# Register loops of eight heads for the load and relay programs of an attention-times-values kernel

## The chip, the cores and the metric

The kernel runs on one core of one Trainium2 chip. The metric is the device time of one execution in microseconds. Each time quoted is the median of several executions; all were in the undisturbed state (none over 1.5% above the fastest of its kernel) unless said otherwise. In the views of the profile PE is TensorE, DVE VectorE, ACT ScalarE, POOL GpSimd and SP SyncE; L129 is line 129 of the kernel. A load *lands* when its semaphore has counted all of it, and a buffer's *release* is the end of the transposes that read it.

## The reference

```python
def setup_inputs():
    batch, n_heads, seq, head_dim = 8, 12, 1024, 64
    return {
        "attn_weights": np.random.randn(batch, n_heads, seq, seq).astype(np.float32),
        "v": np.random.randn(batch, n_heads, seq, head_dim).astype(np.float32),
    }

def reference(attn_weights, v):
    return np.einsum('bhqs,bhsd->bhqd', attn_weights, v).astype(np.float32)
```

There are 96 products of a 1024 x 1024 matrix of weights with a 1024 x 64 matrix v. The weights alone are 402.65 MB, and each is used once per column of v.

## The kernel before

A *unit* is half the rows of four heads, so the 96 heads make 48 units, and *four* units are eight heads. GpSimd loads a unit's weights as one transfer of 8.39 MB, cast to bf16 on the way, into one of two buffers `abf`. TensorE transposes the unit in sixteen groups, VectorE and ScalarE copy the transposes to `at`, TensorE multiplies them by v, transposes the product back, and the copies of it go to `osb`, from where they are stored. A load for unit n + 2 may be issued when unit n has been transposed. TensorE, VectorE and ScalarE already run register loops; GpSimd and SyncE are written out. The parts that the change touches:

```python
def load_attn(n):                       # on GpSimd
    pieces = [(0, G)] if n < HALVED else [(0, GH), (GH, GH)]
    for g0, gn in pieces:
        pool.dma_start(
            out=abf[n % 2][:, ds(g0, gn)].rearrange("p g s -> p (g s)"),
            in_=attn_q[n // 2][:, ds((n % 2 * G + g0) * S, gn * S)],
        ).then_inc(s_abf[n % 2] if g0 == 0 else s_second[n], 16)
...                                     # cut: load_v, store
load_attn(0)
load_attn(1)
...                                     # cut: constants
for n in range(NU - 2):                 # NU = 48; written out
    q, i = n // 2, n % 2
    if i == 0 and q % 2 == 1 and q + 1 < NV:
        for s in s_sp:
            pool.wait_ge(s, 2 * q + 2)
        load_v((q + 1) // 2)
    pool.wait_ge(s_t[True], (n + 1) * PER_DVE)    # unit n is transposed
    load_attn(n + 2)
    if i == 0 and q % 2 == 0 and 0 < q <= HELD_FROM:
        store_2(q - 2)
```

SyncE waits for each load and passes its landing on to TensorE, which asks for it in the middle of the unit (`s_half`):

```python
for n in range(-2, NU - 2):             # written out
    if n + 2 < HALVED:
        nc.sync.wait_ge(s_abf[n % 2], 16 * ((n + 2) // 2 + 1))
    else:
        nc.sync.wait_ge(s_second[n + 2], 16)
    nc.sync.sem_inc(s_half)
    ...                                 # cut: the same for v (s_vr) and for stores (s_free)
```

Of the kernel before, what the change touches and what calls it, by code (L numbers as in the profile page):

```python
# [10 lines left out]
def kernel(  # L11
# [18 lines left out]
    nc = tc.nc  # L30
# [4 lines left out]
    B, H, Q, S = attn_weights.shape  # L35
# [5 lines left out]
    G = Q // VP // 2  # L41
# [5 lines left out]
    NV = NH // VH  # L47
    NU = 2 * NV


    HELD_FROM = NV - 8
    BY_SYNC = NV - 4

    RING = 5
    NO = 2 * RING

    HALVED = NU - 2

    def slot(q):
        return q % NO  # L60

    attn_q = attn_weights.rearrange("b (hq four) (p r) s -> (b hq) (four p) (r s)", four=VH, p=VP)
    out_q = out.rearrange("b (hq four) (p r) d -> (b hq) (four p) (r d)", four=VH, p=VP)
    out_2 = out.rearrange("b h q d -> (b h) q d").rearrange(
        "(hq two four) (p r) d -> hq (four p) two (r d)", two=2, four=VH, p=VP
    )
    v_2 = v.rearrange("b h q d -> (b h) q d").rearrange(
        "(hq two four) (p r) d -> hq (four p) two (r d)", two=2, four=VH, p=VP
    )

    def on_dve(g):
        return g % 8 in (0, 2, 4, 5, 7)
# [5 lines left out]
    PER_DVE = sum(on_dve(g) for g in range(G))  # L78
    PER_ACT = G - PER_DVE

    with tc.tile_critical(no_gpsimd_drain=True):  # L81
        sem = tc.alloc_semaphore
# [3 lines left out]
        abf = [sb(f"abf{i}", [P, G, S], bf16) for i in range(2)]  # L86
        at = sb("at", [P, G, KW, P, 2], bf16)
        vr = sb("vr", [P, 2, VB, SB * D], bf16)
        vbf = sb("vbf", [P, SB, VH, D], bf16)
        ot = sb("ot", [P, GH, P], fp32)  # L90
        osb = sb("osb", [P, NO, 2 * G, D], fp32)
# [8 lines left out]
        s_abf = [sem(f"s_abf{i}") for i in range(2)]  # L100
        s_second = {n: sem(f"s_second{n}") for n in range(HALVED, NU)}
        s_v0, s_v = sem("s_v0"), sem("s_v")
        s_osb = [sem(f"s_osb{i}") for i in range(2)]
        s_held, s_end = sem("s_held"), sem("s_end")

        s_t = {True: sem("s_t_dve"), False: sem("s_t_act")}
        s_sp = [sem("s_sp_dve"), sem("s_sp_act")]
# [8 lines left out]
        s_out, s_fin = sem("s_out"), [sem("s_fin0"), sem("s_fin1")]  # L116
        s_memset, s_const, s_vr = sem("s_memset"), sem("s_const"), sem("s_vr")

        s_half, s_free = sem("s_half"), sem("s_free")
# [192 lines left out]

        pool = nc.gpsimd

        def load_attn(n):
            pieces = [(0, G)] if n < HALVED else [(0, GH), (GH, GH)]
            for g0, gn in pieces:
# [4 lines that stand above are left out]

        def load_v(iv):
            pool.dma_start(  # L324
                out=vr.rearrange("p two b x -> p two (b x)"), in_=v_2[iv]
            ).then_inc(s_v, 16)

        def store(q, fours, eng, done):
            eng.wait_ge(s_out, 2 * (q + fours) + 1)
            at_slot = osb[:, ds(slot(q), fours)].rearrange("p n r d -> p n (r d)")  # L330
            eng.dma_start(  # L331
                out=out_2[q // 2] if fours == 2 else out_q[q],
                in_=at_slot if fours == 2 else at_slot[:, 0],
                **({"single_packet": True} if eng is pool else {}),
            ).then_inc(done, 16)

        def store_2(q):
            store(q, 2, pool, s_osb[q // 2 % 2] if q < HELD_FROM else s_held)

        load_attn(0)  # L340
        load_attn(1)
        pool.wait_ge(s_memset, 2)
        pool.affine_select(
            out=ident,
            in_=ident,
# [7 lines left out]
        for h in range(VH):  # L353
            pool.wait_ge(s_const, h + 1)
            pool.affine_select(  # L355
                out=spread[ds(h * VP, VP)],
                in_=spread[ds(h * VP, VP)],
# [3 lines left out]
                pattern=[[1, VB], [-1, P]],  # L361
                channel_multiplier=VB,
            ).then_inc(s_const)
        for n in range(NU - 2):
            q, i = n // 2, n % 2
            if i == 0 and q % 2 == 1 and q + 1 < NV:
                for s in s_sp:
                    pool.wait_ge(s, 2 * q + 2)
                load_v((q + 1) // 2)
            pool.wait_ge(s_t[True], (n + 1) * PER_DVE)  # L370
            load_attn(n + 2)
            if i == 0 and q % 2 == 0 and 0 < q <= HELD_FROM:
                store_2(q - 2)
        for q in range(HELD_FROM, BY_SYNC, 2):
            store_2(q)
        pool.drain()


# [4 lines left out]
        for two, p0, pn in ((0, 0, P), (1, 0, 96), (1, 96, 22), (1, 118, 10)):  # L383
            nc.sync.dma_start(  # L384
                out=v32_2[ds(p0, pn), two], in_=v_2[0][ds(p0, pn), two]
            ).then_inc(s_v0, 16)
        nc.sync.sem_inc(s_free, RING)
        for n in range(-2, NU - 2):

            if n + 2 < HALVED:  # L390
                nc.sync.wait_ge(s_abf[n % 2], 16 * ((n + 2) // 2 + 1))
            else:
                nc.sync.wait_ge(s_second[n + 2], 16)
            nc.sync.sem_inc(s_half)
            if n >= 0 and n % 2 == 0:
                q = n // 2
                if q % 2 == 1 and q + 1 < NV:
                    nc.sync.wait_ge(s_v, 16 * ((q + 1) // 2))
                    nc.sync.sem_inc(s_vr, 2)
                if q % 2 == 1 and 1 < q <= HELD_FROM:  # L400
                    nc.sync.wait_ge(s_osb[(q - 3) // 2 % 2], 16 * ((q - 3) // 4 + 1))
                    nc.sync.sem_inc(s_free)
        store(NV - 4, 2, nc.sync, s_end)
        store(NV - 2, 1, nc.sync, s_end)
        rows = osb[:, slot(NV - 1)].rearrange("p (u half j) d -> p u half j d", u=2, half=2)
# [3 lines left out]
        for k in range(2):  # L409
            nc.sync.wait_ge(s_fin[k], 1)  # L410
            js = ds(4 * k, 4)
            nc.sync.dma_start(out=outs[:, 1, :, js], in_=rows[:, 1, :, js]).then_inc(s_end, 16)
        for k in range(2):
            nc.sync.wait_ge(s_osb[k], 16 * (HELD_FROM // 4))
        nc.sync.wait_ge(s_held, 16 * (BY_SYNC - HELD_FROM) // 2)
        nc.sync.wait_ge(s_end, 16 * 5)

# [29 lines left out]
```

## Time and profile before

| | before |
|---|---|
| time, median of 6 | 1055.07 us (1054.65 to 1055.70) |
| profile's span | 1053.1 us |
| busy share: TensorE, VectorE, ScalarE, GpSimd | 70%, 37%, 39%, 4% |
| bytes over the span | 452.99 MB, 430 GB/s |
| weight load, from issue to landing | 33.3 us |

Second, the row of instruction fetches among the DMA queues, which is to be compared after:

```profile
q14 instruction: 3, 0.02, 0.0%
```

### The profile page before, as it was taken

Reading aid. Unit: us, or ns where it says so; the run is one execution under the profiler, and the core shown is the slowest. Engines: PE = TensorE matmul, PEld = TensorE weight load, DVE = VectorE, ACT = ScalarE, POOL = GpSimd, SP = SyncE. Lnnn points to the kernel's source line nnn. Section 1 sums busy time; section 2 is a strip of 40 time slices with the busy share of each in tenths; the row PEclk is TensorE's granted clock in tenths of the full one; section 3 lists DMA queues with packets and bytes.
Section 4 is the critical chain, followed back from the end, with each engine's and each line's share of the span. In section 5 each row is a group of like instructions: output and inputs, shape, how many; then the busy total and the mean of one; then the engine's idle time right before and its main releaser. Section 6 shows DMA issues by size and latency. Waiting matters only on the chain.

```text
span 1053.1 us, 16530 instructions
## 1 busy us (share of the span) xinstructions
PE 738.0 (70%) x6920; PEld 692.4 (66%) x6920; DVE 388.8 (37%) x582; ACT 410.3 (39%) x493; POOL 45.1 (4%) x80
## 2 busy tenths in 40 slices
PE   0787677676697568667768757765776866875885
PEld 0686676565686567656668657765766866865874
DVE  0453343333353234333334324433333433532542
ACT  0354344433353334333335334433333533533542
POOL 1000000000000000000000000000000000000000
PEclk9989888898798888889879888888887987988998
DMA  9999999999999999999999999999999999999998
GB/s 235 224 217 218 218 244 219 219 214 249 231 214 251 215 219 258 217 219 230 243 217 210 259 217 218 259 219 219 248 217 217 218 211 225 219 208 230 206 216 339
DMA packets 14330, 240.19 MB, mean 228 GB/s; under 512 B 1269, under 2 KB 1781, under 8 KB 4725
## 3 DMA queue, kind: packets, MB, share of 16 engines
q0 software_dynamic: 12912, 233.84, 99.1%
q1 hardware_dynamic: 1413, 6.29, 1.5%
q8 instruction: 2, 0.03, 0.0%
q14 instruction: 3, 0.02, 0.0%
HBM read 427.82 MB, written 25.17 MB: 430 GB/s over the span
## 4 chain that ended last, share of the span: by engine, by line
DMA 75%; PE 22%; issue 1%; DVE 0%; SPq 0%; ACT 0%; POOL 0%; DVEq 0%
DMA abf<-in_attn_weights_dram 72%; PE bank L129 21%; DMA osb<-in_v_dram 3%; PE bank L171 1%; PE bank L156 0%; DVE vbf L229 0%; SPq L384 0%; PE bank L144 0%; DVE at L250 0%; DVE osb L236 0%; ACT ot L262 0%; POOL abf L318 0%; DVEq L249 0%; DVE vr L308 0%; DVEq L283 0%
## 5 line engine op out<-in xcount | busy, mean ns | idle before, releaser
L129 PE MATMUL bank<-ident,abf 128*128 128x128 f32 x3072 | 454.1, 318 | 273.6 <-DMA abf<-in_attn_weights_dram 264.4
L129 PEld LDWEIGHTS bank<-ident,abf 128*128 128x128 f32 x3072 | 444.2, 214 | 286.8 <-DMA abf<-in_attn_weights_dram 276.2
L250 DVE COPY at<-bank 128x1024 bf16<-128x1024 bf16 x480 | 320.4, 689 | 463.8 <-PE bank L129 460.0
L250 ACT COPY at<-bank 128x1024 bf16<-128x1024 bf16 x288 | 288.8, 1012 | 419.9 <-PE bank L129 419.9
L171 PE MATMUL bank<-at,vbf 128*64 128x256 bf16 x3072 | 215.0, 278 | 0.0
L171 PEld LDWEIGHTS bank<-at,vbf 128*64 128x64 bf16 x3072 | 196.8, 108 | 13.4 <-DVE at L250 4.0
L262 ACT COPY ot<-bank 128x512 f32<-128x512 f32 x48 | 28.1, 586 | 174.2 <-PE bank L171 174.2
L262 DVE COPY ot<-bank 128x512 f32<-128x512 f32 x48 | 33.2, 692 | 151.3 <-PE bank L171 151.3
L156 PE MATMUL bank<-ident,ot 128*128 128x128 f32 x392 | 52.2, 276 | 32.9 <-DVE vbf L229 32.1
L156 PEld LDWEIGHTS bank<-ident,ot 128*128 128x128 f32 x392 | 43.4, 141 | 45.0 <-DVE vbf L229 43.9
L236 ACT COPY osb<-bank 128x512 f32 (+1 forms) x97 | 52.2, 589 | 27.1 <-PE bank L156 26.3
L318 POOL DMA_DIRECT2D abf<-in_attn_weights_dram x50 | 27.3, 546 | 692.4 <-PE bank L129 691.4
L229 DVE CAST vbf<-bank 128x512 bf16<-128x512 f32 x48 | 30.9, 686 | 6.5 <-PE bank L144 6.5
L229 ACT CAST vbf<-bank 128x512 bf16<-128x512 f32 x48 | 25.8, 589 | 11.8 <-PE bank L144 11.8
L144 PE MATMUL bank<-vr,spread 32*128 32x512 bf16 x384 | 25.8, 377 | 0.0
L324 POOL DMA_DIRECT2D vr<-in_v_dram x11 | 7.8, 706 | 234.9 <-PE bank L144 234.9
L250 ACT ACT_TABLE_LOAD x12 | 15.4, 1283 | 1.3 <-SPq L81 1.1
L144 PEld LDWEIGHTS bank<-vr,spread 32*128 32x128 bf16 x384 | 10.2, 92 | 6.7
L308 DVE CAST vr<-osb 128x4096 bf16<-128x4096 f32 x1 | 2.3, 2294 | 30.4 <-DMA osb<-in_v_dram 30.4
L331 POOL DMA_DIRECT2D out_dram<-osb x10 | 7.2, 717 | 30.4 <-ACT osb L236 30.4
L355 POOL TENSOR_SCALAR_AFFINE_SELECT spread<-spread 32x512 bf16<-32x512 bf16 x4 | 2.5, 631 | 0.6
L236 DVE COPY osb<-bank 128x512 f32<-128x512 f32 x1 | 0.7, 692 | 3.1 <-PE bank L156 3.1
(8 smaller groups left out, 2.1 us busy)
## 6 DMA issues: line engine op xcount, KB each, us to landing
abf<-in_attn_weights_dram POOLq DMA_DIRECT2D x46, 4096.0 KB, 33.3
out_dram<-osb POOLq DMA_DIRECT2D x10, 2048.0 KB, 29.5
vr<-in_v_dram POOLq DMA_DIRECT2D x11, 1024.0 KB, 17.2
abf<-in_attn_weights_dram POOLq DMA_DIRECT2D x4, 2048.0 KB, 24.4
out_dram<-osb SPq DMA_DIRECT2D x1, 2048.0 KB, 13.7
osb<-in_v_dram SPq DMA_DIRECT2D x1, 1024.0 KB
out_dram<-osb SPq DMA_DIRECT2D x1, 1024.0 KB, 15.8
osb<-in_v_dram SPq DMA_DIRECT2D x1, 768.0 KB
```

What stands on the lines that cost most here:

```text
L129: last = pe.matmul(out=pt[g % 4][:, k], lhsT=words[:, k], rhs=ident, is_transpose=True, start=(k == 0), stop=(k == KW - 1),)
L144: last = pe.matmul(out=ps, lhsT=spread[rows, b], rhs=vr[rows, two, b], start=(b == 0), stop=(b == VB - 1),)
L156: last = pe.matmul(out=ps[:, ds(j * P, P)], lhsT=ot[:, j0 + j], rhs=ident, is_transpose=True, start=(j == 0), stop=(j == jn - 1),)
L171: last = pe.matmul(out=outs, lhsT=vbf[:, 2 * kw + par, h], rhs=at[:, ds(half * GH, GH), kw, ds(h * VP, VP), par], start=(n == 0), stop=(n ...
L229: copy(out=vbf[:, :, h], in_=ps.rearrange("p (k d) -> p k d", k=SB)).then_inc(s_vbf[e])
L236: return copy(out=rows.rearrange("p (half j) d -> p j half d", half=2)[:, ds(j0, jn)], in_=ps[:, ds(0, jn * P)].rearrange("p (j half d) -> ...
L250: ins = copy(out=at[:, g].rearrange("c k j two -> c (k j two)"), in_=bank[g % 4].bitcast(bf16),)
L262: copy(out=ot.rearrange("c j (h p) -> c h j p", h=VH)[:, ds(2 * e, 2)], in_=po[e].rearrange("c (h j p) -> c h j p", h=2, j=GH),).then_inc( ...
L318: pool.dma_start(out=abf[n % 2][:, ds(g0, gn)].rearrange("p g s -> p (g s)"), in_=attn_q[n // 2][:, ds((n % 2 * G + g0) * S, gn * S)],).th ...
L324: pool.dma_start(out=vr.rearrange("p two b x -> p two (b x)"), in_=v_2[iv]).then_inc(s_v, 16)
L331: eng.dma_start(out=out_2[q // 2] if fours == 2 else out_q[q], in_=at_slot if fours == 2 else at_slot[:, 0], **({"single_packet": True} if ...
L355: pool.affine_select(out=spread[ds(h * VP, VP)], in_=spread[ds(h * VP, VP)], compare_op=mybir.AluOpType.not_equal, fill=1.0, base=0, patte ...
```

## The change

GpSimd and SyncE get loops of eight heads too, with the load's, store's and v's addresses taken from the loop's count. The first round and the last ones stay written out. The two semaphores of the stores become one, and since two stores in flight must not share one (the prediction names the page), GpSimd now waits for SyncE's count of finished stores ahead of each store of the loop. The core of the diff, with cuts marked:

```diff
-        s_osb = [sem(f"s_osb{i}") for i in range(2)]
+        s_osb = sem("s_osb")
...
+        def load_attn_of(hq, i):
+            pool.dma_start(
+                out=abf[i].rearrange("p g s -> p (g s)"),
+                in_=attn_q[ds(hq, 1), :, ds(i * G * S, G * S)].rearrange("one p x -> (one p) x"),
+            ).then_inc(s_abf[i], 16)
...
+        def pool_eight(t, slot_at, four, three, freed):
+            for n in range(4):
+                if n == 2:
+                    for x in s_sp:
+                        pool.wait_ge(x, four + 4)
+                    load_v(t + 1)
+                pool.wait_ge(s_t[True], three + (n + 1) * PER_DVE)
+                load_attn_of(2 * t + (n + 2) // 2, n % 2)
+                if n == 0 and slot_at is not None:
+                    pool.wait_ge(s_out, four + 1)
+                    pool.wait_ge(s_free, freed)
+                    pool.dma_start(
+                        out=out_2[ds(t - 1, 1)].rearrange("one p two x -> (one p) two x"),
+                        in_=osb[:, ds(slot_at, 2)].rearrange("p n r d -> p n (r d)"),
+                        single_packet=True,
+                    ).then_inc(s_osb, 16)
+
+        pool_eight(0, None, 0, 0, None)
+        with nc.Fori(1, HELD_FROM // 2 + 1, 1, engines=(mybir.EngineType.Pool,)) as it:
+            slot_at = pool.snap((it - 1) % RING * 2)
+            four, three = (pool.snap(it * (4 * x)) for x in (1, PER_DVE))
+            pool_eight(it, slot_at, four, three, pool.snap(it + (RING - 1)))
+        for t in range(HELD_FROM // 2 + 1, NV // 2 - 1):
+            pool_eight(t, None, 4 * t, 4 * t * PER_DVE, None)
...
+        with nc.Fori(1, HELD_FROM // 2, 1, engines=(mybir.EngineType.SP,)) as it:
+            four, eight = (nc.sync.snap(it * x) for x in (32, 16))
+            relays_of(four, eight, (s_osb, eight))
```

`relays_of` holds a round's waits and increments, for four loads, a v and a store, in the order that they had. `HELD_FROM` is 16, so GpSimd's loop has 8 rounds and SyncE's 7.

More of the change, by code (lines that the diff above doesn't have):

```diff
@@ L324, in load_v @@
             pool.dma_start(
-                out=vr.rearrange("p two b x -> p two (b x)"), in_=v_2[iv]
+                out=vr.rearrange("p two b x -> p two (b x)"),
+                in_=v_2[ds(iv, 1)].rearrange("one p two x -> (one p) two x"),
             ).then_inc(s_v, 16)
@@ L335, in store @@
             ).then_inc(done, 16)
-        def store_2(q):
-            store(q, 2, pool, s_osb[q // 2 % 2] if q < HELD_FROM else s_held)
         load_attn(0)
@@ L363 @@
             ).then_inc(s_const)
-        for n in range(NU - 2):
-            q, i = n // 2, n % 2
-            if i == 0 and q % 2 == 1 and q + 1 < NV:
-                for s in s_sp:
-                    pool.wait_ge(s, 2 * q + 2)
-                load_v((q + 1) // 2)
+        def pool_eight(t, slot_at, four, three, freed):
[21 more added lines that the diff above has]
+            pool_eight(t, None, 4 * t, 4 * t * PER_DVE, None)
+        for n in range(NU - 4, NU - 2):
             pool.wait_ge(s_t[True], (n + 1) * PER_DVE)
             load_attn(n + 2)
-            if i == 0 and q % 2 == 0 and 0 < q <= HELD_FROM:
-                store_2(q - 2)
         for q in range(HELD_FROM, BY_SYNC, 2):
-            store_2(q)
+            store(q, 2, pool, s_held)
         pool.drain()
@@ L387, with relay, relays_of @@
         nc.sync.sem_inc(s_free, RING)
-        for n in range(-2, NU - 2):
-            if n + 2 < HALVED:
-                nc.sync.wait_ge(s_abf[n % 2], 16 * ((n + 2) // 2 + 1))
-            else:
-                nc.sync.wait_ge(s_second[n + 2], 16)
-            nc.sync.sem_inc(s_half)
-            if n >= 0 and n % 2 == 0:
-                q = n // 2
-                if q % 2 == 1 and q + 1 < NV:
-                    nc.sync.wait_ge(s_v, 16 * ((q + 1) // 2))
-                    nc.sync.sem_inc(s_vr, 2)
-                if q % 2 == 1 and 1 < q <= HELD_FROM:
-                    nc.sync.wait_ge(s_osb[(q - 3) // 2 % 2], 16 * ((q - 3) // 4 + 1))
-                    nc.sync.sem_inc(s_free)
+        def relay(to, of, n, by=1):
+            nc.sync.wait_ge(of, n)
+            nc.sync.sem_inc(to, by)
+        def relays_of(four, eight, stored):
+            for n in range(4):
+                relay(s_half, s_abf[n % 2], four + 16 * (2 + n // 2))
+                if n == 2:
+                    relay(s_vr, s_v, eight + 16, 2)
+                    if stored is not None:
+                        relay(s_free, *stored)
+        for i in range(2):
+            relay(s_half, s_abf[i], 16)
+        relays_of(0, 0, None)
+        with nc.Fori(1, HELD_FROM // 2, 1, engines=(mybir.EngineType.SP,)) as it:
+            four, eight = (nc.sync.snap(it * x) for x in (32, 16))
+            relays_of(four, eight, (s_osb, eight))
+        for t in range(HELD_FROM // 2, NV // 2 - 1):
+            relays_of(32 * t, 16 * t, None)
+        for n in range(HALVED, NU):
+            relay(s_half, s_second[n], 16)
         store(NV - 4, 2, nc.sync, s_end)
@@ L412 @@
             nc.sync.dma_start(out=outs[:, 1, :, js], in_=rows[:, 1, :, js]).then_inc(s_end, 16)
-        for k in range(2):
-            nc.sync.wait_ge(s_osb[k], 16 * (HELD_FROM // 4))
+        nc.sync.wait_ge(s_osb, 16 * (HELD_FROM // 2))
         nc.sync.wait_ge(s_held, 16 * (BY_SYNC - HELD_FROM) // 2)
```

## The prediction

> **What bounds the kernel now.** I read the busy shares first, then the HBM line and the DMA queues, then the chain that ended last, then the waits of each engine, and last the timeline of GpSimd and TensorE over one group of eight heads. From the page of the kernel before:
>
> ```profile
> PE 738.0 (70%) x6920; PEld 692.4 (66%) x6920; DVE 388.8 (37%) x582; ACT 410.3 (39%) x493; POOL 45.1 (4%) x80
> ...
> DMA  9999999999999999999999999999999999999998
> ...
> HBM read 427.82 MB, written 25.17 MB: 430 GB/s over the span
> ...
> DMA 75%; PE 22%; issue 1%; DVE 0%; SPq 0%; ACT 0%; POOL 0%; DVEq 0%
> ```
>
> No compute engine is full, GpSimd least of all (4%). The DMA row is at nine tenths or more in 39 of 40 slices, and three quarters of the chain is DMA. The bytes are the least the task allows: the weights are 8 x 12 x 1024 x 1024 x 4 B = 402.65 MB, v and the output 25.17 MB each, which gives the 427.82 MB read and 25.17 MB written. So the kernel streams its input once, at 430 GB/s, and nothing can remove a byte.
>
> The waits say the same (engine, line, releaser: us in total, times, longest):
>
> ```profile
> POOL abf L318 <- PE bank L129: 691.4, 35, 37.4
> ...
> PE bank L129 <- DMA abf<-in_attn_weights_dram: 264.4, 45, 28.4
> ```
>
> GpSimd spends most of the span waiting for TensorE to finish with a buffer, so that it may issue the next load. TensorE waits 264.4 / 45 = 5.9 us per unit (half the rows of four heads) for a load. Neither wait alone says which side is late; the timeline of one group of eight heads does. GpSimd's issues (start us, duration us):
>
> ```profile
> 272.82 0.53 POOL L318 DMA_DIRECT2D abf<-in_attn_weights_dram  x1 [22.94 <-PE bank L129]
> 296.87 0.53 POOL L318 DMA_DIRECT2D abf<-in_attn_weights_dram  x1 [23.52 <-PE bank L129]
> 301.20 0.71 POOL L331 DMA_DIRECT2D out_dram<-osb  x1 [3.80 <-ACT osb L236]
> 313.84 0.56 POOL L318 DMA_DIRECT2D abf<-in_attn_weights_dram  x1 [11.93 <-PE bank L129]
> 336.53 0.71 POOL L324 DMA_DIRECT2D vr<-in_v_dram  x1 [22.13 <-PE bank L144]
> 337.23 0.56 POOL L318 DMA_DIRECT2D abf<-in_attn_weights_dram  x1
> ```
>
> TensorE's transposes, each starting as the load before has landed:
>
> ```profile
> 286.21 10.36 PE L129 MATMUL bank<-ident,abf 128*128 128x128 f32 x64 [8.40 <-DMA abf<-in_attn_weights_dram]
> ...
> 305.53 8.02 PE L129 MATMUL bank<-ident,abf 128*128 128x128 f32 x64 [1.11 <-DMA abf<-in_attn_weights_dram]
> ...
> 325.01 9.81 PE L129 MATMUL bank<-ident,abf 128*128 128x128 f32 x64 [6.18 <-DMA abf<-in_attn_weights_dram]
> ...
> 349.17 9.70 PE L129 MATMUL bank<-ident,abf 128*128 128x128 f32 x64 [6.50 <-DMA abf<-in_attn_weights_dram]
> ```
>
> Set each issue against the landing of the load that is in flight at that moment: 286.21 - 272.82 = 13.4 us, 305.53 - 296.87 = 8.7, 325.01 - 313.84 = 11.2, 349.17 - 337.23 = 11.9. That is the slack of an issue: the transfer queue still has **8.7 to 13.4 us** of work when GpSimd adds the next load. An issue that comes later by less than that leaves no hole in the stream. This number decides the case.
>
> The same phase recurs at 184.81 and at 795.50 us, seven groups later, so a group takes 610.69 / 7 = 87.2 us. It moves 4 x 8.39 MB of weights (the page counts a load as 4096 KB because it lands as bf16; it is read as float32), 2.10 MB of v and 2.10 MB of output: 37.75 MB / 87.2 us = 433 GB/s.
>
> **What the Trainium skill says.** "DMA: Bandwidth & Descriptors", section "Where 436 GB/s comes from", puts the ceiling of the 16 ports at 435.2 GB/s and says that HBM traffic usually binds lower, at some 358. The 433 of this trace is far over the second and 0.5% under the first, so I take the first as this kernel's limit. The same page, "Why a DMA increments its semaphore by 16 and not by 1", says that the number of engines of a transfer follows from its slowest dimension that isn't of size 1, and that two transfers in flight on one semaphore can satisfy a wait for the first too early; the second is why the change adds a wait where it merges two semaphores. "Advanced Engine Details and Errata", "Control Flow Timing", gives 51 ns for a branch and 108 ns for a compare and branch; no view of this trace shows one. "Runtime: NRT & Kernel Launch", "Instruction fetch mechanics", warns that a taken branch to a block that isn't held stalls for a fetch. TensorE, VectorE and ScalarE run loops already, and the page of before counts just five instruction packets (0.05 MB), so the loops there don't fetch each round through the visible queues.
>
> **The change, part by part.**
>
> Loads, stores and words of v: the same transfers in the same order. GpSimd issues 46 + 4 loads, 11 of v and 10 stores before; after it is 2 first loads, 11 groups of 4 loads and one of v, four halves, 8 + 2 stores: 50, 11 and 10. Bytes, destination and row lengths (128 rows, the leading dimension of size 1 dropped) stay as they are. Difference 0, if the descriptors come out alike.
>
> Register arithmetic and branches: eight rounds on GpSimd, seven on SyncE. A round has one compare and branch, a handful of values for the waits, and address arithmetic for six transfers on GpSimd. What can be done ahead costs nothing, as the engine waits some 20 us before the next release. What stands between a release and the issue delays it. My estimate: ten operations at the page's 108 ns are 1.1 us; should the issue itself, 0.53 to 0.71 us, double as well, that is 1.8 us. Against a slack of 8.7 us: 0 on the path.
>
> A fetch at the back edge: no duration of one is seen; I allow several us once a round. It falls after the round's last load has been issued, and the next issue is some 23 us away, so 0 again.
>
> SyncE's relays: it waits 1025.7 us in 48 waits, 21.4 us each, for loads to land, and passes each on to TensorE, which needs it only at the ninth of sixteen groups of transposes, half of 8.0 us after it started, so 4 us later. A loop adds tenths of a microsecond. Even a relay that is late delays TensorE first, whose release of the buffer has the 8.7 us behind it.
>
> The new wait on GpSimd, for SyncE's count of stores: in round t it needs that store t - 1 has landed. That was issued some 87 us earlier and landed after a median 29.5 us; SyncE passes it on when unit 4t has landed, and GpSimd asks after TensorE and ScalarE have worked on this unit, some 10 us later. It never blocks: 0. The last round's remaining waits are constants, as before.
>
> What is removed: straight-line instructions, and with them at most the fetch of a few blocks. All five instruction packets together, 0.05 MB at 433 GB/s, are 0.1 us.
>
> The sum: 0 to +0.3 us on 1055.1. The start (both first loads come ahead of the loop) and the tail (the last groups are written out) don't change.
>
> **The rivals.** First, **the issue becomes the bound**: register work or a fetch stall delays issues beyond the slack. To cost 2%, 21.1 us, once in each of eight rounds it would have to be 8.7 + 21.1 / 8 = 11.3 us late; if on each of the 32 loads of the loop, 8.7 + 0.7 = 9.4 us. Nothing in the profile has that size. If it did happen, 1060 to 1080 us. Second, **the transfers differ**: an address out of a register makes other descriptors, or fewer engines work on one. The shapes speak against it, and the queue is software-generated already. If it happened, the whole of the loop runs slower, well over 1100 us. Third, **a gain**: freed instruction memory or an earlier issue. But the stream is gapless: 453 MB at the page's 435.2 GB/s would be an estimated 1041 us, only 1.1% under the span of 1053.1, so a gain of 2% is out of reach even for a perfect kernel. An earlier issue only lengthens the queue: the load lands at the same time.
>
> **Range and chances.** I choose 1055.3 us, the time before and a trace of added work. The three runs before spread over 0.7 us. What I don't know is whether a different phase of the loads against the stores shifts the stream slightly; some 4 us either way covers that: 1051 to 1059. Within 2% has 97%; slower 2%, for the first two rivals; faster 1%, for something I can't see.
>
> **What would show it.** In the changed kernel's profile: HBM bytes the same, 430 GB/s within 1, the DMA row full. Loads of 4096 KB x46 with about 33 us to landing; if the issue is later, this time gets *shorter* by as much while the span stays, which is the sign of slack being used. POOL x80 and busy near 45 us, unless a register-addressed issue takes longer. Issue against preceding landing in one group: still over 6 us. TensorE's waits for loads near 264 us. No long wait of GpSimd for SyncE before a store. The prediction would be wrong if the DMA row shows holes at the start of each round (first rival), or if packets are more and smaller (second).

## More of the kernel before

The prediction shows the views that carry the argument. Two more are needed for the comparison. First, a piece of the profile's chain of work, followed back from the last instruction, around one issue (start us, duration us, what):

```profile
262.02 10.51 PE bank L129 x64
272.53 0.29 issue
272.82 32.66 DMA abf<-in_attn_weights_dram
```

TensorE's last transpose ends at 272.53 us, and GpSimd's load starts 0.29 us later.

## The result, and the profile after

The changed kernel took 1054.87 us (six runs, 1054.57 to 1055.06), against 1055.07 us of the kernel before in the same rounds. The ratio is 0.9998, with a 95% interval from 0.9985 to 1.0011. Ratios in this text are those of mean times over the same rounds, without the profiled execution, which the medians include; so they are not quite the ratios of the quoted medians. The time is the same, and the prediction of 1055.3 us was 0.4 us off.

From the page of the changed kernel, the lines that answer to those of before:

```profile
PE 737.4 (70%) x6920; PEld 691.7 (66%) x6920; DVE 388.3 (37%) x582; ACT 410.1 (39%) x493; POOL 45.0 (4%) x80
...
q0 software_dynamic: 12912, 233.84, 99.0%
...
q14 instruction: 2, 0.02, 0.0%
HBM read 427.82 MB, written 25.17 MB: 430 GB/s over the span
...
abf<-in_attn_weights_dram POOLq DMA_DIRECT2D x46, 4096.0 KB, 33.2
```

Busy times, packets, bytes and the time to landing are those of before. The only trace of the shorter program is one instruction fetch fewer. Then the waits (engine, line, releaser: us in total, times, longest):

```profile
PE bank L129 <- DMA abf<-in_attn_weights_dram: 269.5, 45, 29.4
...
POOL out_dram L386 <- ACT osb L236: 28.6, 7, 4.1
```

TensorE waits 5 us more for loads in total, over 45 waits. The stores wait for ScalarE's copies as before; SyncE, whose count of stores GpSimd now waits for, is in none of GpSimd's waits after the start. The cost of the loop is seen in the chain, around the same issue as before:

```profile
262.62 9.74 PE bank L129 x64
...
272.38 0.04 POOLq L317
...
272.45 0.03 POOLq L317
272.48 0.47 issue
272.95 0.03 POOLq L393
272.98 33.11 DMA abf<-in_attn_weights_dram
```

From TensorE's release to the load are 0.62 us where there were 0.29. Two register operations of 0.07 us in all stand in between (POOLq is GpSimd's sequencer), and then 0.47 us in which nothing is recorded. As it ends, the sequencer goes on to its next instruction (line 393), so in these 0.47 us it was presumably busy with the load. The timeline gives 0.64 us for the same interval by another end of the last transpose; I use 0.64 and 0.30 below, a difference of 0.34 us. The issue itself didn't get longer. The changed kernel's load line by itself (nanoseconds: shortest/median/longest):

```profile
L317 POOL DMA_DIRECT2D abf<-in_attn_weights_dram x44: 528/531/573, 42.0 to 958.0; - x44
L317 POOLq FUSED_REGOPS  x32: 42/48/72, 121.6 to 795.0; - x32
```

Before, the median was 531 ns too. Of the loop's 32 loads, 24 came 0.34 to 0.39 us later after their release. The other eight, the fourth of each round, are issued behind a v and came 0.16 us later, with the v. That is 9.3 us in all, and the time didn't move. (The expectations below reckon with 32 x 0.34 = 10.9 us, which is too much by this count.) Issue and preceding landing are still over 6 us apart in the group that the prediction read, 13.8, 9.0, 10.9 and 11.1 us where 13.4, 8.7, 11.2 and 11.9 had been; the tightest is

```profile
297.11 0.53 POOL L317 DMA_DIRECT2D abf<-in_attn_weights_dram  x1 [23.60 <-PE bank L129]
```

```profile
306.13 8.02 PE L129 MATMUL bank<-ident,abf 128*128 128x128 f32 x64 [1.84 <-DMA abf<-in_attn_weights_dram]
```

The experiments ask where these 9.3 us went, and whether the slack that I had read off is really what took them.

### The profile page after: what moved, and what is told of

The parts are those of the page before. It is cut to its first block, busy times and chain, and to the rows that moved or that the text cites. A ratio compares the mean times of both kernels' runs of the same rounds, so it can differ in the third digit from the quotient of the medians.

```text
span 1053.4 us, 16746 instructions
## 1 busy us (share of the span) xinstructions
PE 737.4 (70%) x6920; PEld 691.7 (66%) x6920; DVE 388.3 (37%) x582; ACT 410.1 (39%) x493; POOL 45.0 (4%) x80
## 3 DMA queue, kind: packets, MB, share of 16 engines
q0 software_dynamic: 12912, 233.84, 99.0%
## 4 chain that ended last, share of the span: by engine, by line
DMA 75%; PE 21%; issue 3%; POOL 0%; POOLq 0%; DVE 0%; SPq 0%; ACT 0%; DVEq 0%
DMA abf<-in_attn_weights_dram 72%; PE bank L129 20%; DMA osb<-in_v_dram 3%; PE bank L171 0%; PE bank L156 0%; SPq L412 0%; PE bank L144 0%; POOLq L317 0%; POOL vr L331 0%; DVE at L250 0%; DVE osb L236 0%; ACT ot L262 0%; POOL abf L317 0%; POOL abf L325 0%; POOLq L393 0%
## 5 line engine op out<-in xcount | busy, mean ns | idle before, releaser
L262 DVE COPY ot<-bank 128x512 f32<-128x512 f32 x48 | 33.2, 691 | 151.4 <-PE bank L171 151.4
L229 ACT CAST vbf<-bank 128x512 bf16<-128x512 f32 x48 | 25.8, 589 | 11.9 <-PE bank L144 11.9
## 6 DMA issues: line engine op xcount, KB each, us to landing
abf<-in_attn_weights_dram POOLq DMA_DIRECT2D x46, 4096.0 KB, 33.2
```

The costliest lines, as they stand in the source:

```text
L229: copy(out=vbf[:, :, h], in_=ps.rearrange("p (k d) -> p k d", k=SB)).then_inc(s_vbf[e])
L262: copy(out=ot.rearrange("c j (h p) -> c h j p", h=VH)[:, ds(2 * e, 2)], in_=po[e].rearrange("c (h j p) -> c h j p", h=2, j=GH),).then_inc( ...
```

## The experiments

Twelve kernels ran. The results were correct, but for one.

**Is the stream of bytes the bound?** The eight stores of the loop write only an eighth of their bytes, so the result is wrong.

```diff
-  out=out_2[ds(t - 1, 1)].rearrange("one p two x -> (one p) two x"),
-  in_=osb[:, ds(slot_at, 2)].rearrange("p n r d -> p n (r d)"),
+  out=out_2[ds(t - 1, 1)].rearrange("one p two x -> (one p) two x")[:, :, ds(0, 4 * D)],
+  in_=osb[:, ds(slot_at, 2)].rearrange("p n r d -> p n (r d)")[:, :, ds(0, 4 * D)],
```

> The changed kernel with a wrong result on purpose: the eight stores of the loop write an eighth of their bytes, 0.26 of 2.10 MB. Theory (the stream of bytes is the bound): 8 x 1.84 MB = 14.7 MB fewer at 433 GB/s, 33.9 us less, about 1021 us. Rival (the hand-over of the two weight buffers sets the pace, and the stores ride along in gaps): within 5 us of 1055.

It took 1019.74 us, ratio 0.9668, so 35 us less against 33.9 expected. Its page:

```profile
HBM read 427.82 MB, written 10.49 MB: 431 GB/s over the span
```

The bytes fell and the rate stayed. Stores don't ride along in gaps; every byte takes its time, so the stream is the bound.

**What if an issue has no slack at all?** Two kernels get the same wait more: GpSimd issues the load of unit n + 2 only when unit n + 1 has landed. One is the kernel before, the other the changed one.

```diff
   pool.wait_ge(s_t[True], (n + 1) * PER_DVE)
+  if n < NU - 4:
+      pool.wait_ge(s_abf[(n + 1) % 2], 16 * ((n + 1) // 2 + 1))
   load_attn(n + 2)
```

> The kernel before with one wait more on GpSimd: each of the loads of units 2 to 45 (44 loads) is issued only when the load ahead of it has landed, so no issue has slack. Theory (the queue always holds a load, which is why issue time is hidden): every load now leaves a hole from landing to first byte, some 2 us by the fixed cost that the Trainium skill states plus 0.3 us of issue, so about 44 x 2.3 = 101 us more, less what v and the stores fill: 1120 to 1160 us. Rival (the kernel is held by something other than the stream, so the depth of the queue doesn't matter): 1055 us.

The 2 us are those of the Trainium skill, "DMA: Bandwidth & Descriptors", section "Anatomy of one DMA", whose fixed cost of about 2.0 us is setup and completion of a transfer together, and not only what follows a landing.

```diff
   pool.wait_ge(s_t[True], three + (n + 1) * PER_DVE)
+  pool.wait_ge(s_abf[(n + 1) % 2], eights + 16 * ((n + 1) // 2 + 1))   # eights = 32 t
   load_attn_of(2 * t + (n + 2) // 2, n % 2)
```

> The changed kernel with the same wait more. In its profile three loads of a round are issued 0.63 to 0.66 us after TensorE's release, in the kernel before 0.29 to 0.31. Theory (the loop's register work is real and only hidden by slack): with the slack gone it shows, 32 loop loads x 0.34 = 10.9 us over exposed_straight. Rival (the register work overlaps with the wait and costs nothing even without slack): 0 to 2 us over exposed_straight.

The first took 1147.81 us (ratio 1.0887), 94 us more: the load that is always queued is worth 94 us. That is 2.1 us for each of the 44 loads, near the expected 2.3, but this is partly luck. By the packets of the trace, only 25 of the 44 loads leave a hole in which no packet moves, of 2.05 us each, 51 us together: 0.29 us from the last packet to the landing, 0.53 us to the issue and 1.23 us from there to the load's first packet. At the others v or a store fills it. Another 14 us go where some of the 16 DMA engines stand idle, and 26 us because packets of the weights took longer than before. The second took 1151.19 us (ratio 1.0915), so the loop costs 0.28% of 1055 us, 3.0 us, where I had expected 10.9. The expectation was too high, and the chains say why. First exposed_straight, then exposed_loop:

```profile
330.68 0.02 issue
330.70 0.02 POOLq L372
330.72 0.49 issue
331.21 23.43 DMA abf<-in_attn_weights_dram
```

```profile
331.63 0.02 issue
331.65 0.07 POOLq L317
331.72 0.03 issue
331.75 0.03 POOLq L317
331.78 0.47 issue
332.25 0.02 POOLq L385
332.27 23.24 DMA abf<-in_attn_weights_dram
```

The straight program needs 0.53 us here too, not 0.29. A second wait puts one instruction ahead of the load (line 372, 0.02 us), and then the same silence of almost half a microsecond follows. So most of the 0.34 us isn't register arithmetic. It looked like the load's own decoding, which in the kernel before would run ahead, because there the load itself carries its only wait (no other instruction is recorded between release and issue). That was a new theory, so it was tried: in exposed_loop the last wait is moved onto the load instruction, behind the register operations.

```diff
-  pool.wait_ge(s_abf[(n + 1) % 2], eights + 16 * ((n + 1) // 2 + 1))
-  load_attn_of(2 * t + (n + 2) // 2, n % 2)     # shortened: load_attn_of returns its load
+  count = pool.to_reg(eights + 16 * ((n + 1) // 2 + 1))
+  load = load_attn_of(2 * t + (n + 2) // 2, n % 2)
+  load.wait_op(s_abf[(n + 1) % 2], count, "sem-ge")
```

> exposed_loop with the wait for the load ahead carried by the load instruction itself, so that the register operations stand before the wait. In exposed_loop the issue came 0.67 to 0.75 us after the landing, of which the page shows 0.1 us of register operations and 0.47 to 0.58 us without an instruction; exposed_straight had 0.54 us with the same 0.49 us silence after a separate wait. Theory (the silence is the load's own decoding, which runs ahead when the load itself waits): 0.3 us after the landing, 44 x 0.4 = 16 us less than exposed_loop, about 1135 us, under exposed_straight too. Rival (the silence belongs to the issue wherever the wait stands): only the 0.1 us of register operations go, 1147 us.

It took 1140.94 us (ratio 1.0818): 0.97% or 10.2 us less than exposed_loop, and 7.3 us less than exposed_straight. The rival's 1147 us is out; of the 16 us some 60% came, because again only 25 of the 44 loads leave a hole without packets: it shrank from 2.16 us on average in exposed_loop to 1.80, which is 8.9 of the 10.2 us. The landing as TensorE acts on it, and the issue after it (TensorE's line, then GpSimd's, of one moment):

```profile
282.36 9.90 PE L129 MATMUL bank<-ident,abf 128*128 128x128 f32 x64 [6.28 <-DMA abf<-in_attn_weights_dram]
```

```profile
282.60 0.56 POOL L317 DMA_DIRECT2D abf<-in_attn_weights_dram  x1 [11.79 <-DMA abf<-in_attn_weights_dram]
```

The issue comes 0.24 us after TensorE's start, and exposed_loop had 332.27 - 331.67 = 0.60 us by the same count. So the silence can be hidden by letting the load carry the wait. That it is decoding fits, but no view names it.

**Does this help where there is slack?** The same edit in the changed kernel, on its wait for the release.

> The changed kernel with the wait for the release carried by the load itself. Theory: the issue comes 0.3 us after the release as in the kernel before instead of 0.64 us, and the time doesn't move, 1054 to 1056 us, as the 0.34 us lay in the slack. Rival (the 0.34 us have a share of the time that something else gave back): 32 x 0.34 = 11 us less, 1044 us.

Its issues come 0.29 us after the release again, for instance 313.23 against 304.92 + 8.02 = 312.94 us in its timeline. The time was 1054.63 us, ratio 0.9998 with an interval from 0.9981 to 1.0015. The 8.5 us that the issues gained (the fourth of each round still comes with its v) bought nothing that can be measured, as the theory said, and the rival's 1044 us is far out.

**Is it one half of the change against the other?** In one kernel SyncE's relays are written out and GpSimd keeps its loop, in the other the opposite:

```diff
 # only_sync
-  with nc.Fori(1, HELD_FROM // 2 + 1, 1, engines=(mybir.EngineType.Pool,)) as it:
-      ...
+  for t in range(1, HELD_FROM // 2 + 1):
+      pool_eight(t, (t - 1) % RING * 2, 4 * t, 4 * t * PER_DVE, t + (RING - 1))
```

> The changed kernel with SyncE's relays written out as before; GpSimd keeps its loop and its one store semaphore. Theory (all of the loop's cost lies in slack): 1054.6 to 1055.2 us, no difference from both kernels. Rival (a cost of GpSimd's loop, made up by a gain of SyncE's): over 1056 us here and under 1054 us in only_sync.

> The changed kernel with GpSimd's eight rounds written out (same semaphores, same wait for SyncE's count of stores); SyncE keeps its loop. Theory: 1054.6 to 1055.2 us. Rival as for only_pool: under 1054 us.

Both had a median of 1055.34 us, beside 1055.14 us of the kernel before; the ratios are 1.0002 (0.9989 to 1.0016) and 1.0000 (0.9986 to 1.0014). Both missed the stated band by 0.1 us, as the kernel before almost did in these rounds. No loss made up by a gain shows, within the 1.7 us that these intervals leave.

**How much delay does the slack really take?** GpSimd is given memsets between the release and the issue of each of 44 loads. The first attempt put a drain after each of ten small memsets, to keep them in order:

```diff
   pool.wait_ge(s_t[True], three + (n + 1) * PER_DVE)
+  for _ in range(10):
+      pool.memset(idle, 0.0)
+      pool.drain()
   load_attn_of(2 * t + (n + 2) // 2, n % 2)
```

> The changed kernel with ten small memsets, each with a drain, on GpSimd between the release of a buffer and the issue of each load (44 loads). A look to see how long the ten take, between 3 and 10 us by guess. Theory (8.7 us or more of slack, of which 0.34 is used): the time stays within 2 us of 1055 if the delay is under 8 us. Rival (the slack is much smaller than the timeline suggests): 44 x the delay, over 100 us more.

This failed as a measurement: 1467.97 us, one run, state unknown. GpSimd's timeline shows why:

```profile
302.56 0.52 POOL L374 MEMSET idle<- 32x512 bf16 x1 [1.61 <-PE bank L130]
327.36 5.57 POOL L374 MEMSET idle<- 32x512 bf16 x9 [24.28 <-issue]
```

After the first memset comes a silence of 24.28 us, and only then the other nine. The drain ends when GpSimd's own transfers in flight have landed: two loads later the memsets resume at 389.23 us, and TensorE starts on the landed load at 389.13 us. So every load was issued onto an empty queue, 6.2 us or more after the landing ahead of it. The next ones use larger memsets, chained by a semaphore, two and four of them:

```diff
   pool.wait_ge(s_t[True], three + (n + 1) * PER_DVE)
+  for j in range(2):                       # 4 in linger_4, 1 in linger_1
+      pool.wait_ge(s_idle, count + j)      # count from the loop's count
+      pool.memset(idle, 0.0).then_inc(s_idle)      # idle: 128 x 4096 bf16
+  pool.wait_ge(s_idle, count + 2)
   load_attn_of(2 * t + (n + 2) // 2, n % 2)
```

> The changed kernel with two memsets of 128 x 4096 on GpSimd, chained by a semaphore, between the release of a buffer and the issue of each of 44 loads; by guess 4 us each, so a delay D of 8 us. Theory: a load's slack of 8.7 to 13.4 us takes all of it, 1055 to 1060 us. Rival (the slack is smaller than read): over 1100 us.

> The same with four memsets, D of 16 us by guess. Theory, two buffers: from one load of a buffer to its next there are two loads' times, which must hold transposes of some 9.5 us, 0.6 us of issue, D, and 22.6 us from issue to landing on an empty queue (exposed runs). The stream needs 2 x 21.8 = 43.6 us, so D shows from 10.9 us on, and then at half: 44 x (16 - 10.9) / 2 = 112 us more, about 1167 us. Rival, as the prediction reckoned (each load's delay beyond its slack of on average 11.3 us in full): 44 x 4.7 = 207 us more, about 1262 us.

The delay D is the time from release to issue less the 0.64 us of the changed kernel. In linger_2 it is 7.1 us, in linger_4 14.3 us. linger_2 took 1086.82 us (ratio 1.0318, 34 us more), where 1055 to 1060 had been expected. linger_4 took 1181.89 us (ratio 1.1201, 127 us more), near the 112 us of the theory that two buffers halve an excess and far from the 207 of the rival. But a theory whose threshold is passed 4 us early isn't right. In linger_2, the tightest issue of a group and the landing of the load ahead of it, GpSimd first, then TensorE:

```profile
311.66 0.53 POOL L318 DMA_DIRECT2D abf<-in_attn_weights_dram  x1 [0.66 <-POOL idle L377]
```

```profile
312.67 8.02 PE L130 MATMUL bank<-ident,abf 128*128 128x128 f32 x64 [1.06 <-DMA abf<-in_attn_weights_dram]
```

Of the 9 us one is left, as planned; yet 34 us over 11 groups are lost, 3.1 us a group. Either the slack can't be used to its end, or the memsets themselves disturb the transfers. Half the dose and then the same memsets without delay were to tell this apart.

> The changed kernel with one memset of 128 x 4096 (3.54 us in linger_2) between release and issue of each of 44 loads, some 4 us with the chaining. linger_2's trace shows the stream run dry 2.5 us ahead of the moment at which TensorE sees a load as landed, so the tightest load's slack of 8.7 to 9.0 us is worth only some 6 us. Theory: 4 us still fit, 1054 to 1056 us, and the memsets themselves don't slow the transfers. Rival (linger_2 lost its 32 us to memsets that disturb the transfers, in proportion to their number): half of it, 1071 us.

linger_1 took 1068.85 us, with runs from 1059.30 to 1070.26, ratio 1.0108 (1.0065 to 1.0151), so 11 us more for D = 3.6 us; why one of the four runs lost only 4 us is not known. That was near the rival's number and not the theory's. In the last kernel the two memsets of linger_2 stand behind the load and the store, where GpSimd would have waited anyway:

```diff
-  linger(idled + n * 2)                    # ahead of load_attn_of
   load_attn_of(2 * t + (n + 2) // 2, n % 2)
   ...                                      # the store, in the quarter round that has one
+  linger(idled + n * 2)
```

> linger_2 with its two memsets moved behind the load and the store of a quarter round, where GpSimd would otherwise wait: the same 88 memsets and chains, but no issue is delayed. It tells apart what cost linger_1 its 13 us and linger_2 its 32 us. If the delay of the issue did (also below the slack that the timeline shows): 1055 to 1057 us. If the memsets disturb the transfers: about 1087 us, as linger_2.

It took 1055.15 us, beside 1054.94 of the kernel before (ratio 1.0002, 0.9988 to 1.0016). The same memsets cost nothing:

```profile
296.76 0.53 POOL L318 DMA_DIRECT2D abf<-in_attn_weights_dram  x1 [16.48 <-PE bank L130]
...
302.08 7.10 POOL L377 MEMSET idle<- 128x4096 bf16 x2
314.25 0.56 POOL L318 DMA_DIRECT2D abf<-in_attn_weights_dram  x1 [5.07 <-PE bank L130]
```

So it is the delay of the issue that costs, and it does so while the timeline still shows slack. In linger_1 the tightest issue of the group at 300 us has 5.4 us left:

```profile
304.45 0.53 POOL L318 DMA_DIRECT2D abf<-in_attn_weights_dram  x1 [0.65 <-POOL idle L377]
```

```profile
309.81 8.02 PE L130 MATMUL bank<-ident,abf 128*128 128x128 f32 x64 [1.82 <-DMA abf<-in_attn_weights_dram]
```

| kernel | delay D of 44 issues, us | ratio to before | extra, us |
|---|---|---|---|
| changed kernel | 0 (24 of its issues 0.34 later than before) | 0.9998 | 0 |
| linger_1 | 3.6 | 1.0108 | 11 |
| linger_2 | 7.1 | 1.0318 | 34 |
| linger_4 | 14.3 | 1.1201 | 127 |
| busy_2 (memsets, no delay) | 0 | 1.0002 | 0 |

The extra is the ratio less 1, times 1055 us. Where it goes can be read from the packets of the traces, in part. The 5,888 packets of 32 KB that carry the weights take 2434 ns on average in the trace of before and 2458 ns in linger_1's; over 16 engines that is 5888 x 24 ns / 16 = 9 us, most of the 13.0 us by which the profiled span is longer. Those that overlap a memset take 2433 ns, so the slow ones are elsewhere. Of the 200 that took over 2.6 us (the longest 4.2), 184 belong to one load in each group, that of unit 4t + 2, whose issue is the tightest and which the store follows. Before, there were 32, and 29 of them there too.

The other part is plain. At the start, where the kernel before has only 3.7 us between the issue for unit 2 and the landing ahead of it, linger_1's issue came 0.1 us after the landing, and the engines stood idle for 3.1 us on average. Nowhere else in linger_1 did they stand idle for over 0.2 us around the start of a load; within the loop 4.6 us or more were left. In linger_2 the two parts are 13 us of idle engines, most of them at units 4t + 2, and 17 us of slower packets. Two things eat up the slack there. A load's first packet starts 1.2 us after its issue at the soonest, and the 16 engines don't end together: the first of them reported the load ahead up to 2.9 us before the last, whose report is the landing. Why packets slow down while the queue is merely shorter, no run here shows; that stays open.

## Why the prediction was right, point by point

- **The bound.** Right. short_stores gave back 35 us for 14.7 MB, as 433 GB/s has it.
- **The transfers stay the same.** Right: 12,912 packets, the same bytes and 33.2 us to landing. The second rival didn't come. I had said that a later issue would shorten the time to landing by as much; 33.3 to 33.2 us is too small a change to show it, but linger_1's 29.0 us and linger_2's 26.1 us do.
- **Register arithmetic and branches.** The estimate was 1.1 us for ten operations, and up to 1.8 us with a doubled issue. Measured: 0.34 to 0.39 us for 24 loads and 0.16 us for eight, and two register operations are under 0.1 us of it; the issue's duration stayed at 0.53 us. The estimate named the wrong cause too: exposed_straight and exposed_on_load show that most of it is a silence ahead of the load which goes when the load carries the wait. Nor is it right that no view shows a branch: the view of line 196 in the trace of before has 36 compare-and-branches on TensorE, of 77 to 223 ns.
- **A fetch at the back edge.** None shows. The page has one fetch fewer, and the load behind the back edge comes as soon after its release as the others: 0.66 us in the round at 297 us, beside 0.64 us for the next two.
- **SyncE's relays.** Right. SyncE still waits 1022.4 us in 48 waits; TensorE waits for it twice, 3.9 us in all against 5.4 before; only_sync is as fast as before.
- **The new wait for stores.** Right. SyncE never is the releaser of a store.
- **The slack of 8.7 to 13.4 us.** The subtraction was right for the group that I read, and over the loop's 32 loads the trace of before has 8.6 to 14.5 us; but some loads of the first and last groups have less (3.7 us at unit 2). The use of it was wrong. "An issue that comes later by less than that leaves no hole in the stream" made of the slack a threshold, counted to the landing, which is the report of the slowest engine. At the loop's tightest load (296.87 us) the first engine reported after 7.0 us, its last packet had ended some 0.3 us earlier, and a new load needs 1.2 us to its first packet: by estimate 5.5 us until an engine runs dry, and not 8.7. And the cost sets in before that: 3.6 us of delay cost 11 us, of which slower packets are some 9. The first rival's sum, that 9.4 us on each load would be needed for 2%, is too high: 2% (21 us) lies between D = 3.6 and 7.1 us. Had the loop delayed every issue by 5 us, the time would by this table have left the stated range.
- **What this leaves for the change.** If linger_1's cost held in proportion down to small delays, 11 us / (44 x 3.6 us) = 0.07, the loop's 9.3 us would cost 0.7 us. The interval of the result, some 1.4 us either way, can't tell this from nothing. Shown is that the cost is at most some 1.2 us (the upper end of the interval, 1.0011); wait_on_load, with most of the delay taken back, is at most 2.0 us faster than the kernel before (its lower end, 0.9981).

The gain that one might have hoped for isn't there for the reason given: GpSimd and SyncE wait for most of the span, and the stream that they feed already moves 430 GB/s.

## What to carry to other kernels

Shortening the programs of engines that mostly waited paid nothing here, where a stream of transfers is the bound; its risk is only that issues come later, so compare release and issue before and after. Distance between an issue and the landing ahead of it is a reserve, but not a free one: test it with a delay of a few microseconds before building on it, and check with the same work off the path that it is the delay which costs. Where an issue is on the path, let the transfer itself carry the last wait and put the register operations ahead of it.

## What the Trainium skill lacked or had wrong

- "DMA: Bandwidth & Descriptors" says nothing on which instruction carries the wait; "Perfetto Trace Analysis", "DMA Instruction — SWDGE (GPSIMD)", has decoding ahead of the semaphore wait, but no time for it. An issue that carries its own wait came 0.24 to 0.30 us after its release, one behind a separate wait or register operation 0.53 to 0.69 us; with no slack the move was worth 10.2 us (exposed_loop against exposed_on_load).
- "DMA: Bandwidth & Descriptors", "Anatomy of one DMA", has a fixed cost of about 2.0 us per transfer. It doesn't say how long the engines stand still between two loads of which the second is issued when the first has landed: 2.05 us in exposed_straight, of which 0.53 us are the issuing engine's. Nor does it say that a shorter queue, not yet empty, slows packets: some 9 us in linger_1.
- The same page, "Where 436 GB/s comes from", says that the HBM side, some 358 GB/s, binds transfers between HBM and SBUF. That doesn't hold for one core alone, as the page's own measurement of 425 GB/s for 16 MB shows too: here one core moved 430 GB/s over the whole span, so the ceiling of the ports, 435.2 GB/s in the same section, is the one to reckon with.
- "Advanced Engine Details and Errata", "Control Flow Timing", has one figure, 108 ns, for a compare and branch. GpSimd's eight in the changed kernel are recorded with 40 to 50 ns, and 0.16 to 0.17 us pass from the start of one to the next recorded instruction; TensorE's at line 196 have a median of 169 ns.
- No page that I read says that a drain on GpSimd waits for the transfers which it has issued: 24.28 us of silence in linger_10.
